# Projecting queries, keys and values in four groups, one per mLSTM head, with sample rows per head

## The chip, the cores and the metric

The kernel runs as one program on one core of one Trainium2 chip. The metric is the device time of one execution in microseconds (us). Work is shared between TensorE (PE in the profile; PEld is its weight load), VectorE (DVE), ScalarE (ACT), GpSimd (POOL, here mostly a second issuer of transfers) and SyncE (SP, which issues the weight loads).

## The reference

One layer of a hybrid decoder, for 256 prompt tokens and 8 sample tokens of one step each. One combined projection feeds two groups, an RG-LRU recurrence and an mLSTM with four heads; their outputs go through `w_out`. Then come a cross attention over 256 memory tokens and a gated feed-forward part.

```
xn = rmsnorm(x, g_mix)
z = xn @ w_in                      # rgx | rgg | q | k | v | o | i | f
xr, conv_new = causal_conv(z[..., OFF_RGX:OFF_RGG], ...)
h_rg, h_last = rglru(xr, r, i, lam, h0)          # a scan over time
y_rg = rmsnorm(h_rg * gelu(z[..., OFF_RGG:OFF_Q]), g_rg_out)
h_ml, C_new, n_new, m_new = mlstm(q, k * DK**-0.5, v, logi, logf, C0, n0, m0)
y_ml = rmsnorm(h_ml, g_ml_out) * sigmoid(z[..., OFF_O:OFF_I])
x = x + concat([y_rg, y_ml]) @ w_out
x = x + CrossAttn(rmsnorm(x, g_xa), mem k/v)
x = x + SwiGLU(rmsnorm(x, g_ffn))
y = rmsnorm(x, g_final)
```

For a prompt, a head of the mLSTM computes the products of its queries and keys (128 wide), weights them by gates, and multiplies with its values (256 wide). For a sample token it updates a 128 x 256 state C = dec C + k v, a normaliser n = dec n + k, and reads both with q. All states are outputs too.

## The kernel before

**Tiles.** The model dimension lies on the partitions, the 264 token columns (256 prompt, 8 sample) on the free axis. A weight block is 16 tiles of 128 x 128. Precision comes from splitting: ACT copies half a block (8 tiles) to fp32r (the high part, written `w<-raw` by ACT), DVE subtracts it from the raw data (the low part, `w<-raw,w` by DVE), and each tile is then used in three matmuls of 264 columns: high x high, high x low, low x high. So a block is a *step* of 48 matmuls in two *halves* of 24, and each half needs one pass of ACT and one of DVE. There are four buffers for split halves, so a split can begin when PE has left the half four before.

**Steps.** A list `steps` holds the blocks in the order in which PE takes them; the main loop near the end of the kernel runs over it. Steps 0 to 3 are the first four rgx blocks at once (a quarter of the depth each), 4 to 7 the other rgx blocks, 8 the gates (half as long), 9 to 16 the four q blocks and then the four k blocks, 17 to 24 the eight v blocks, 25 to 32 rgg, 33 to 40 o, 41 to 56 `w_out`. Then come `w_q`, the memory's keys and values, `w_o` and the feed-forward blocks. A block of `w_out` takes its first eight tiles from the recurrence (`yrg`), the last eight from the mLSTM (`yml`); the products with `yml` of its first blocks are asked for after the mLSTM's norm, so PE can take `yrg` halves of several blocks first.

**Accumulators.** A step ends with an evacuation (`evac_...`) of a PSUM bank that DVE or ACT reads. Of the eight banks `bank` gives four to `mm`, the steps, and four to `ax`, everything else; the first four rgx blocks use three `ax` and one `mm`.

**Side work.** All that is not a step is a generator, registered by `side(generator, prio)` and advanced by `pump` after each step. A `yield STEP` ends a generator's turn until the next step, `yield` with a number only offers a stop. `pump` goes through them by priority number and stops one that used DVE or ACT once that engine's planned clock is at the clock of PE plus a slack. `finish` runs them without such a limit. The planner then lays the recorded instructions out on each engine by a model of their times; each engine executes its own list in order. The side generators here:

- `rg_gen` (prio 0, from step 7): convolution, gates, exponentials and scans of the recurrence; a rgg step needs it to be done.
- `ml_gates` (0): gate values of the mLSTM, from step 8.
- `ml_prompt` (2), `ml_values` (2), `ml_heads` (2): transposed keys and the weighted q x k product of a head (`Pm`, with keys scaled in `kw`), transposed values, and the product of `Pm` and the values.
- `ml_sample` (3): the sample states. It writes k and q rows of the sample tokens to a scratch buffer `scr` in memory and reads them back broadcast over the partitions (`B<-scr`, with `c0T` for the old state). ACT forms products of k and v (`dw`), DVE the new state (`B<-B,bcs,dw`) and its dot products with q (`ds<-B,B`).
- `ml_norm` (6, from step 24): waits for heads and samples, sums over partitions by a matmul with ones (`ax<-ssum,ones`), finds the scale, scales `hT` (`B<-B,B` TENSOR_SCALAR), transposes it and forms `yml`.
- `mem_gen` (7, from step 40): the norm of the memory tokens, with an inverse root over a 128 x 256 tile in `rstd_wide`.

`evac_qk(7)`, the last k, starts `ml_sample`, `ml_prompt`, `ml_values` and `ml_heads`. `ml_prompt` transposes the keys of all heads into two banks and copies them to SBUF before the first head.

Of the kernel before, what the change touches and what calls it, by code (L numbers as in the profile page):

```python
# [17 lines left out]
P = 128  # L18
# [77 lines left out]
def layer_kernel(ctx: ExitStack, tc, xT, memT, vec, wrg, w_in, w_out, w_q, w_k, w_v, w_o,  # L96
# [236 lines left out]
    def bank(tag="mm"):  # L333
        return psm.tile([P, 512], F32, tag=tag, bufs=4, name=nm(tag))
# [390 lines left out]
    def evac_qk(j):  # L725
        def f(ps):
            if j == 0:
                ml["qk"] = Arr(8)
            if j < 4:
                dve.tensor_mul(halves(ml["qk"](j)), unturn(ps[:, :N]), halves(rstd))  # L730
            else:
                dve.scalar_tensor_tensor(halves(ml["qk"](j)), unturn(ps[:, :N]), KSCALE, halves(rstd),
                                         op0=OP.mult, op1=OP.mult)
# [40 lines left out]
    def ml_prompt():  # L774
        qk = ml["qk"]
        yield STEP
# [7 lines left out]
        while "gates" not in ml or not ml["gates"].done:  # L784
            yield STEP
        R = ml["R"]
        M = R(6)[:, :T]
        for h in range(H):
            sel = ident[:, h: h + 1].to_broadcast([P, P])
            bc = bank("ax")  # L790
            pe.matmul(bc[:, :T], sel, M, start=True, stop=True)
            sps = bank("ax")
# [4 lines left out]
            E, Pm, kw = w[:, 0:384], w[:, 384:768], ml["kb"][:, h].rearrange("p t d -> p (t d)")  # L797
# [12 lines left out]
            yield 1.0  # L810
            ml["pn"] = h + 1
# [44 lines left out]
    def ml_sample():  # L856
# [3 lines left out]
        ks, qs = qk.tile(1)[:, :, T:N], qk.tile(0)[:, :, T:N]  # L860
        sc, Dg = bcs[:, :, 0:8], bcs[:, :, 8:16]
        x = ltmp(64)
        kd, qc = (x[:, o: o + 32].rearrange("p (h b) -> p h b", b=NS) for o in (0, 32))
        dve.tensor_mul(kd, ks, Dg)
        dve.tensor_copy(qc, qs)
        n0 = V("n0", 0, 32).rearrange("p (h b) -> p h b", b=NS)
        dve.tensor_mul(snew, n0, sc)
        dve.tensor_add(snew, snew, kd)
        pool_e.dma_start(o_sn, snew)

        dve.tensor_mul(ssum[:, 1], snew, qc)
        yield 0.6
        yield STEP
        ps = bank("ax")
        pe.transpose(ps[0:64, 128:256], x, ident)
        yield STEP
        rows = ltmp(128)
        act.activation(rows[0:64, :], ps[0:64, 128:256], AF.Copy)
        scr = drm.tile([64, P], F32, name="scr")
        pool_e.dma_start(scr, rows[0:64, :])  # L880
        yield 0.5
        def fetch(h, b4):
            C, kq = B([P, 4, 2, P]), B([P, 2, 4, P])
            pool_e.dma_start(C, c0T[h, :, b4 * 4: b4 * 4 + 4])
            for j in range(2):
                r0 = j * 32 + h * 8 + b4 * 4
                src = scr[r0: r0 + 4, :].rearrange("b d -> (b d)")
                pool_e.dma_start(kq[:, j].rearrange("p b d -> p (b d)"), src.partition_broadcast(P))
            return C, kq

        ahead = fetch(0, 0)
        yield STEP
        for h in range(H):
            while ml.get("vn", 0) < 2 * h + 2 or "last" not in ml:
                yield STEP
            for b4 in range(2):
                C, kq = ahead
                n = 2 * h + b4 + 1
                if n < 2 * H:
                    ahead = fetch(n // 2, n % 2)  # L900
# [94 lines left out]
    first = [bank("ax"), bank("ax"), bank("ax"), bank()]  # L995
# [9 lines left out]
    def evac_first(_):  # L1005
        for n in (3, 0, 1, 2):
# [450 lines left out]
    for i, (src, cols, pef, evf, need) in enumerate(steps):  # L1457
# [174 lines left out]
```

## Time and profile before

| what | value |
|---|---|
| median of 3 runs | 1449.08 us (1449.05 to 1451.44) |
| the profiled execution | 1449.35 us |
| its span | 1447.4 us |
| mean granted TensorE clock | 0.999 |
| ACT busy | 793.9 us, 55% of the span |
| all DMA | 329.17 MB, 227 GB/s |

The execution's time is 1.95 us longer than its span, which begins and ends with its first and last instruction. "Busy" counts the instructions of an engine; where PE is busy in nearly the whole span, what matters is whether its matmuls follow each other at the pace of its long undisturbed stretches. In a timeline a row is a start, a length, engine, line, operation, operands, a count, and in brackets the idle time before it with what ended it. Names are those of the program's buffers: `w` a split half, `raw` its data, `mm` and `ax` accumulators, `B` and `t` working tiles. L61 is a line of a helper through which nearly all instructions are recorded, so groups are told apart by their names. A length in a timeline includes some overlap with the next instruction; differences of starts give the pace.

### The profile page before, as it was taken

Reading aid. Unit: us, or ns where it says so; the run is one execution under the profiler, and the core shown is the slowest. Engines: PE = TensorE matmul, PEld = TensorE weight load, DVE = VectorE, ACT = ScalarE, POOL = GpSimd, SP = SyncE. Lnnn points to the kernel's source line nnn. Section 1 sums busy time; section 2 is a strip of 40 time slices with the busy share of each in tenths; the row PEclk is TensorE's granted clock in tenths of the full one; section 3 lists DMA queues with packets and bytes.
Section 4 is the critical chain, followed back from the end, with each engine's and each line's share of the span. In section 5 each row is a group of like instructions: output and inputs, shape, how many; then the busy total and the mean of one; then the engine's idle time right before and its main releaser. Section 6 shows DMA issues by size and latency. Waiting matters only on the chain.

```text
span 1447.4 us, 29983 instructions
## 1 busy us (share of the span) xinstructions
PE 1432.6 (99%) x11987; PEld 1407.3 (97%) x11987; DVE 1046.6 (72%) x2007; ACT 793.9 (55%) x1286; POOL 127.8 (9%) x203
## 2 busy tenths in 40 slices
PE   9999999999999999999999999999999999999997
PEld 9999999999999999899999999999999999999997
DVE  7966798998899999977676665555656655556564
ACT  7678785765556666655544444434444443444463
POOL 0001220000225433300000000000000000000000
PEclk9999999999999999999999999999999999999999
DMA  9645897548799887856555555555555555555573
GB/s 288 235 174 184 295 372 272 179 173 276 277 336 376 322 306 258 340 172 216 193 196 196 192 201 192 197 196 192 200 192 195 199 192 198 193 193 200 164 240 126
DMA packets 100764, 329.17 MB, mean 227 GB/s; under 512 B 11056, under 2 KB 19936, under 8 KB 100624
## 3 DMA queue, kind: packets, MB, share of 16 engines
q1 hardware_dynamic: 84336, 271.95, 54.1%
q0 software_dynamic: 15424, 54.22, 10.1%
q8 instruction: 93, 1.52, 0.4%
q10 hardware_dynamic: 864, 1.09, 0.2%
q14 instruction: 47, 0.39, 0.1%
HBM read 314.36 MB, written 12.86 MB: 226 GB/s over the span
## 4 chain that ended last, share of the span: by engine, by line
PE 56%; DVE 1%; issue 1%; DMA 0%; POOL 0%; ACT 0%; DVEq 0%; POOLq 0%; ACTq 0%
PE mm L61 56%; PE ax L61 1%; DVE B L61 1%; DVE dw L61 0%; DMA o_v<-B 0%; POOL ds L1182 0%; DVE w L61 0%; ACT B L61 0%; DVE c L61 0%; ACT dw L61 0%; DVE t L61 0%; ACT ds L61 0%; DVEq L1609 0%; ACT c L61 0%; DVEq L61 0%
## 5 line engine op out<-in xcount | busy, mean ns | idle before, releaser
L61 PE MATMUL mm<-B,w 128*128 128x264 f32 (+1 forms) x10960 | 1282.2, 279 | 1.8 <-DVE w L61 1.7
L61 PEld LDWEIGHTS mm<-B,w 128*128 128x128 f32 x10960 | 1261.5, 189 | 9.9 <-DVE w L61 2.3
L61 DVE TENSOR_TENSOR w<-raw,w 128x1024 fp32r<-128x1024 f32 (+1 forms) x522 | 624.4, 1198 | 303.5 <-ACT w L61 302.7
L61 ACT ACTIVATE w<-raw 128x1024 fp32r<-128x1024 f32 (+1 forms) x522 | 534.9, 1028 | 512.2 <-PE mm L61 347.8
L61 PE MATMUL mm<-w,B 128*128 128x512 f32 x384 | 86.9, 380 | 0.1
L61 PEld LDWEIGHTS mm<-w,B 128*128 128x128 f32 x384 | 70.6, 189 | 9.8 <-DVE w L61 0.5
L1521 POOL TENSOR_TENSOR B<-B,rstd 128x264 f32<-128x264 f32 x4 | 2.8, 738 | 802.9 <-ACT rstd L61 802.9
L61 DVE TENSOR_TENSOR t<-mm,rstd 128x264 f32<-128x264 f32 x96 | 41.4, 432 | 28.4 <-PE mm L61 28.3
L61 DVE SCALAR_TENSOR_TENSOR B<-B,dw 128x256 f32<-128x256 f32 x128 | 55.0, 483 | 3.2 <-ACT dw L61 3.0
L61 DVE TENSOR_TENSOR xres<-xres,mm 128x264 f32<-128x264 f32 (+1 forms) x81 | 34.3, 425 | 27.0 <-PE mm L61 27.0
L61 DVE SCALAR_TENSOR_TENSOR dw<-B,qsm,dw 128x256 f32<-128x256 f32 x96 | 48.6, 511 | 2.6 <-ACT dw L61 1.8
L61 PE MATMUL ax<-B,B 128*128 128x256 f32 (+3 forms) x272 | 44.9, 305 | 1.1 <-DVE B L61 1.0
L1182 POOL TENSOR_TENSOR ds<-dw,ds 128x256 fp32r<-128x256 f32 x32 | 35.4, 1106 | 106.8 <-ACT ds L61 106.7
L61 PEld LDWEIGHTS ax<-B,B 128*128 128x128 f32 x272 | 37.9, 191 | 3.8 <-DVE B L61 1.6
L61 ACT ACTIVATE B<-xres,vecs 128x264 fp32r<-128x264 f32 (+1 forms) x64 | 32.2, 503 | 4.2 <-DVE xres L61 2.7
L61 ACT ACTIVATE dw<-B,qsm 128x256 f32<-128x256 f32 x32 | 16.2, 508 | 27.0 <-issue 13.9
L1171 POOL DMA_DIRECT2D B<-kcT x32 | 17.3, 541 | 139.6 <-DVE B L61 126.5
L61 ACT ACTIVATE t<-xres 128x264 f32<-128x264 f32 (+1 forms) x53 | 21.1, 409 | 15.3 <-DVE xres L61 15.2
L61 ACT ACTIVATE dw<-B,B 128x128 f32<-128x128 f32 x64 | 21.2, 393 | 11.2 <-DMA B<-scr 7.9
L61 DVE SCALAR_TENSOR_TENSOR B<-xres,vecs,B 128x264 fp32r<-128x264 f32 x48 | 23.4, 490 | 4.1 <-ACT B L61 4.1
L61 ACT ACTIVATE dw<-ax,dw 128x256 f32<-128x256 f32 x32 | 15.1, 471 | 19.3 <-DVE dw L61 18.3
L61 ACT ACTIVATE B<-t 128x264 fp32r<-128x264 f32 (+1 forms) x60 | 24.1, 409 | 2.1 <-DVE t L61 2.1
(176 smaller groups left out, 679.0 us busy)
## 6 DMA issues: line engine op xcount, KB each, us to landing
raw<-w_gu SPq DMA_DIRECT2D x176, 512.0 KB, 3.6
raw<-w_d SPq DMA_DIRECT2D x80, 512.0 KB, 3.6
raw<-w_in SPq DMA_DIRECT2D x74, 512.0 KB, 5.2
raw<-w_out SPq DMA_DIRECT2D x32, 512.0 KB, 3.7
raw<-w_q SPq DMA_DIRECT2D x32, 512.0 KB, 6.2
B<-kcT POOLq DMA_DIRECT2D x32, 512.0 KB, 8.8
B<-vcT POOLq DMA_DIRECT2D x32, 512.0 KB, 9.9
raw<-w_k SPq DMA_DIRECT2D x32, 512.0 KB, 5.0
```

The lines of the kernel that those rows point to most:

```text
L61: return f(*a, **k)
L1171: pool_e.dma_start(kc, kcT[h, b])
L1182: pool_e.tensor_sub(ws[:, 1], acc, ws[:, 0].bitcast(F32))
L1521: e.tensor_mul(st["y"](c), st["y"](c), r)
```

## The change

- The eight banks are divided into three `mm` and five `ax`; the first four rgx blocks are all in `ax`. At step 7 the evacuation of step 4, which is alone in `mm` by then, is put ahead of the three others that are waiting.
- Steps 9 to 24 are in the order q0 k0 v0 v1, q1 k1 v2 v3, q2 k2 v4 v5, q3 k3 v6 v7.
- The first k starts the side generators. The last k did so before.
- Sample rows are formed per head by a new generator, `ml_rows` (prio 2): five DVE operations on 8 columns, a transpose to 16 x 128, a copy by ACT and a transfer to the head's part of `scr`. Before, one such chain worked on 32 columns and 64 rows. `ml_sample` waits for a head's rows (`rn`) before it fetches them.
- `ml_prompt` waits for each head's key, transposes it into the second half of the bank that holds the head's gate row, and `kw` is scaled from there. The copies of all keys are gone.
- `ml_heads` has one more `yield STEP` between `Pm` and the product with the values.

The diff, in its core:

```
-        return psm.tile([P, 512], F32, tag=tag, bufs=4, name=nm(tag))
+        return psm.tile([P, 512], F32, tag=tag, bufs=3 if tag == "mm" else 5, name=nm(tag))
...
-            if j == 7:
+            ml["kn"] = j - 3
+            if j == 4:
+                side(ml_rows(), 2)
                 ml["sg"] = side(ml_sample(), 3)
                 side(ml_prompt(), 2)
                 side(ml_values(), 2)
...
-        kt, ml["kb"] = B([P, 2, H, P]), B([P, H, 2, P])
-        for tb in range(2):
-            ps = bank("ax")
-            for h in range(H):
-                pe.transpose(ps[:, h * P: h * P + P], qk(4 + h)[:, tb * P: tb * P + P], ident)
-            act.activation(kt[:, tb].rearrange("p h d -> p (h d)"), ps, AF.Copy)
...
+        for h in range(H):
+            while ml["kn"] <= h:
+                yield STEP
             yield STEP
...
+            bc, sps = bank("ax"), bank("ax")
+            kt = bc[:, T:].rearrange("p (t d) -> p t d", t=2)
+            pe.matmul(bc[:, :T], ident[:, h: h + 1].to_broadcast([P, P]), M, start=True, stop=True)
+            for tb in range(2):
+                pe.transpose(kt[:, tb], k[:, tb * P: tb * P + P], ident)
...
-            act.activation(kw[:, 0:P], kt[:, 0, h, :], AF.Copy, scale=E[:, 255:256])
-            act.activation(kw[:, P:T], kt[:, 1, h, :], AF.Copy, scale=E[:, 383:384])
+            for tb in range(2):
+                e = 255 + 128 * tb
+                act.activation(kw[:, tb], kt[:, tb], AF.Copy, scale=E[:, e: e + 1])
...
             while min(ml.get("pn", 0), ml.get("vtn", 0)) <= h:
                 yield STEP
             yield STEP
+            yield STEP
...
+    def ml_rows():
         while not ml["gates"].done:
             yield STEP
         qk = ml["qk"]
...
+        for h in range(H):
+            while ml["kn"] <= h:
+                yield STEP
+            x = ctile(2 * NS)
+            kd, qc = x[:, 0:NS], x[:, NS:]
+            dve.tensor_mul(kd, qk(4 + h)[:, T:N], bcs[:, h, NS:])
+            dve.tensor_copy(qc, qk(h)[:, T:N])
+            dve.tensor_mul(snew[:, h], V("n0", NS * h, NS), bcs[:, h, 0:NS])
+            dve.tensor_add(snew[:, h], snew[:, h], kd)
+            dve.tensor_mul(ssum[:, 1, h], snew[:, h], qc)
+            yield 0.3
+            yield STEP
+            ps = bank("ax")
+            pe.transpose(ps[0: 2 * NS, 0:P], x, ident)
+            yield STEP
+            rows = ltmp(P)[0: 2 * NS]
+            act.activation(rows, ps[0: 2 * NS, 0:P], AF.Copy)
+            pool_e.dma_start(scr[h], rows)
+            ml["rn"] = h + 1
+            yield 0.2
         pool_e.dma_start(o_sn, snew)
...
+                    while ml["rn"] <= n // 2:
+                        yield STEP
                     ahead = fetch(n // 2, n % 2)
...
-    first = [bank("ax"), bank("ax"), bank("ax"), bank()]
+    first = [bank("ax") for _ in range(4)]
...
-    for j in range(8):
-        proj(w_in[9 + j], rx, evac_qk(j))
-    for j in range(8):
-        proj(w_in[17 + j], rx, evac_v(j))
+    for h in range(H):
+        for j in (h, 4 + h):
+            proj(w_in[9 + j], rx, evac_qk(j))
+        for j in (2 * h, 2 * h + 1):
+            proj(w_in[17 + j], rx, evac_v(j))
...
+        if i == 7:
+            pend.insert(0, pend.pop(1))
```

What this moves is not written in the diff but comes out of the planner. Three places of the instruction lists show it, each before and after.

The first is PE at the turn into `w_out`. Before, `mm_3693` is block 1 and `mm_3843` block 2; `w_3629` is block 1's first half and `w_3632` its second, `B_3671` the high part of the first `yml` tile, and `ax` the transposes of the heads.

```order
L61 MATMUL mm_3693<-B_3321,w_3629 128x264
L61 MATMUL mm_3693<-B_3320,w_3629 128x264
L61 MATMUL ax_3718<-ident,B_2063 128x128 x4
L61 MATMUL ax_3731<-ident,B_2257 128x128 x4
L61 MATMUL ax_3746<-ident,B_2257 128x128 x4
L61 MATMUL mm_3635<-B_3671,w_3569 128x264
L61 MATMUL mm_3693<-B_3671,w_3632 128x264
L61 MATMUL mm_3843<-B_3245,w_3687 128x264
```

In the changed kernel `mm_3661`, `mm_3704` and `mm_3916` are blocks 0, 1 and 2, `w_3698` is the first half of block 2, and `B_3738` and `B_3739` are the high and low part of the first `yml` tile; `ax_3887` is the sum of the memory's norm.

```order
L61 MATMUL mm_3916<-B_3334,w_3698 128x264
L61 MATMUL mm_3916<-B_3333,w_3698 128x264
L61 MATMUL ax_3731<-ident,B_2212 128x128 x4
L61 MATMUL ax_3746<-ident,B_2212 128x128 x4
L61 MATMUL ax_3759<-ident,B_2628 128x128 x4
L61 MATMUL ax_3774<-ident,B_2628 128x128
L61 MATMUL ax_3887<-lt_3787,ones 128x256
L61 MATMUL ax_3774<-ident,B_2628 128x128 x3
L61 MATMUL mm_3661<-B_3738,w_3570 128x264
L61 MATMUL mm_3704<-B_3738,w_3658 128x264
L61 MATMUL mm_3916<-B_3738,w_3701 128x264
L61 MATMUL mm_3661<-B_3739,w_3570 128x264
```

The first products with `yml` stood after the first half of block 1 and were followed by the first half of block 2. They now stand after the first half of block 2, behind all transposes and the memory's sum.

The second place is DVE at the same turn. Before, `B_2063` and `B_2257` are the heads' `hT`, `B_3409` the scale, `B_3080` and `B_3412` the o gates, and `B_3672` the low part of the first `yml` tiles.

```order
L61 TENSOR_TENSOR nums<-nums,B_3409 128x4x8 x2
L61 TENSOR_SCALAR B_2063<-B_2063,B_3409 128x256 x4
L61 TENSOR_SCALAR B_2257<-B_2257,B_3409 128x256 x4
L61 TENSOR_TENSOR B_3080<-B_3080,nums 128x8 x3
L61 TENSOR_TENSOR B_3412<-mm_3572,rstd 128x264
L61 TENSOR_TENSOR B_3080<-B_3080,nums 128x8
L61 TENSOR_TENSOR B_3412<-B_3412,nums 128x8 x3
L61 TENSOR_TENSOR w_3632<-raw_3535,w_3632 128x8x128
L61 TENSOR_TENSOR B_3412<-B_3412,nums 128x8
L61 TENSOR_TENSOR B_3080<-B_3080,ax_3664 128x256 x2
L61 TENSOR_TENSOR w_3687<-raw_3621,w_3687 128x8x128
L61 SCALAR_TENSOR_TENSOR B_3672<-B_3080,vecs,B_3671 128x264 x2
```

After, from the same scaling on, `hT` is `B_2212` and `B_2628`, and the gates are `B_3094` and `B_3429`; `w_3910` is the first half of block 3.

```order
L61 TENSOR_SCALAR B_2212<-B_2212,B_3499 128x256 x4
L61 TENSOR_SCALAR B_2628<-B_2628,B_3499 128x256 x4
L61 TENSOR_TENSOR B_3094<-B_3094,nums 128x8 x4
L61 TENSOR_TENSOR B_3429<-B_3429,nums 128x8 x4
L61 TENSOR_TENSOR B_3094<-B_3094,ax_3731 128x256
L61 TENSOR_TENSOR w_3910<-raw_3686,w_3910 128x8x128
L61 TENSOR_TENSOR B_3094<-B_3094,ax_3731 128x256
L61 TENSOR_TENSOR B_3094<-B_3094,ax_3746 128x256 x2
L61 TENSOR_TENSOR B_3429<-B_3429,ax_3759 128x256 x2
L61 TENSOR_SCALAR t_3889<-ax_3887 128x256
L61 TENSOR_TENSOR B_3429<-B_3429,ax_3774 128x256 x2
L61 SCALAR_TENSOR_TENSOR B_3739<-B_3094,vecs,B_3738 128x264 x4
```

Some rows on, `lt_3834` is the memory's inverse root, `B_3690` to `B_3696` the memory tokens, and `w_3913` the second half of block 3.

```order
L61 TENSOR_TENSOR t_3890<-lt_3834 128x256
L61 SCALAR_TENSOR_TENSOR t_3890<-t_3890,t_3889 128x256
L61 SCALAR_TENSOR_TENSOR lt_3834<-t_3890,lt_3834 128x256
L61 TENSOR_TENSOR B_3690<-B_3690,lt_3834 128x256 x4
L61 TENSOR_TENSOR B_3692<-B_3692,lt_3834 128x256 x4
L61 TENSOR_TENSOR B_3694<-B_3694,lt_3834 128x256 x4
L61 TENSOR_TENSOR xres<-xres,mm_3661 128x264
L61 TENSOR_TENSOR B_3696<-B_3696,lt_3834 128x256 x3
L61 TENSOR_TENSOR xres<-xres,mm_3704 128x264
L61 TENSOR_TENSOR B_3696<-B_3696,lt_3834 128x256
L61 TENSOR_TENSOR w_3913<-raw_3688,w_3913 128x8x128
```

Additions of all gates with their transposes, then the memory's root and its sixteen products, now stand between the splits of block 3's halves; before, the memory's sums began behind the rows shown, and its products came later still.

The third place is ACT while the recurrence runs. Before, `lt_1801` is the row copy of all heads, `B_1539` and `B_1616` are tiles of the recurrence, `B_1707` the copied keys and `dw` the sample products.

```order
L61 ACTIVATE B_1539<-B_1539 128x264 x3
L61 ACTIVATE B_1616<-B_1616 128x264 x3
L61 ACTIVATE B_1707<-ax_1709 128x512
L61 ACTIVATE lt_1801<-ax_1715 64x128
L61 ACTIVATE w_1806<-raw_1693 128x8x128
L61 ACTIVATE w_1809<-raw_1695 128x8x128
L61 ACTIVATE B_1616<-B_1616 128x264
L61 ACTIVATE hlast<-B_1867 128x36
L61 ACTIVATE B_1707<-ax_1789 128x512
L61 ACTIVATE B_1625<-ax_1795 128x2x256
L61 ACTIVATE dw_1982<-B_1882,B_1636 128x128 x2
L61 ACTIVATE dw_2077<-B_1882,B_1636 128x128 x2
```

After, `lt_1581` is the row copy of the first head, `B_1568`, `B_966` and `B_1661` are tiles of the recurrence, `B_1507` is the first head's prompt weight, and `B_1192` its scaled keys.

```order
L61 ACTIVATE lt_1581<-ax_1498 16x128
L61 ACTIVATE B_966<-B_966,rgc 128x264
L61 ACTIVATE B_1568<-B_1568,ones 128x264
L61 ACTIVATE B_966<-B_966,rgc 128x264
L61 ACTIVATE B_1568<-B_1568,ones 128x264
L61 ACTIVATE B_966<-B_966,rgc 128x264
L61 ACTIVATE B_1568<-B_1568,ones 128x264
L61 ACTIVATE B_1507<-B_1507 128x384
L61 ACTIVATE w_1598<-raw_1482 128x8x128
L61 ACTIVATE B_1192<-ax_1500,B_1507 128x128 x2
L61 ACTIVATE w_1601<-raw_1484 128x8x128
```

A few functions of the recurrence later (`B_1661` and `B_1320` are its tiles too) the first sample products `dw` follow.

```order
L61 ACTIVATE B_966<-B_966,rgc 128x264
L61 ACTIVATE B_1568<-B_1568,ones 128x264
L61 ACTIVATE B_1320<-B_1320,rgc 128x264
L61 ACTIVATE B_1661<-B_1661,ones 128x264
L61 ACTIVATE dw_1677<-B_1593,B_1197 128x128 x2
```

The first head's rows, prompt weights and sample products have moved ahead of, and in between, functions of the recurrence that stood before them.

More of the change, by code (lines that the diff above doesn't have):

```diff
@@ L730, in f @@
                 dve.tensor_mul(halves(ml["qk"](j)), unturn(ps[:, :N]), halves(rstd))
-            else:
-                dve.scalar_tensor_tensor(halves(ml["qk"](j)), unturn(ps[:, :N]), KSCALE, halves(rstd),
-                                         op0=OP.mult, op1=OP.mult)
-            if j == 7:
+                return
+            dve.scalar_tensor_tensor(halves(ml["qk"](j)), unturn(ps[:, :N]), KSCALE, halves(rstd),
+                                     op0=OP.mult, op1=OP.mult)
+            ml["kn"] = j - 3
+            if j == 4:
+                side(ml_rows(), 2)
                 ml["sg"] = side(ml_sample(), 3)
@@ L775, in ml_prompt @@
         qk = ml["qk"]
-        yield STEP
-        kt, ml["kb"] = B([P, 2, H, P]), B([P, H, 2, P])
-        for tb in range(2):
-            ps = bank("ax")
-            for h in range(H):
-                pe.transpose(ps[:, h * P: h * P + P], qk(4 + h)[:, tb * P: tb * P + P], ident)
-            act.activation(kt[:, tb].rearrange("p h d -> p (h d)"), ps, AF.Copy)
+        ml["kb"] = B([P, H, 2, P])
+        while not ml["gates"].done:
             yield STEP
-        while "gates" not in ml or not ml["gates"].done:
+        M = ml["R"](6)[:, :T]
+        for h in range(H):
+            while ml["kn"] <= h:
+                yield STEP
             yield STEP
[L786 to L792, printed above, removed]
-            q, k = qk(h), qk(4 + h)
+            q, k = qk(h), qk(4 + h)
+            bc, sps = bank("ax"), bank("ax")
[3 more added lines that the diff above has]
+                pe.transpose(kt[:, tb], k[:, tb * P: tb * P + P], ident)
             pe.matmul(sps[:, 0:256], k[:, 0:P], q[:, 0:T], start=True, stop=True)
@@ L854, in layer_kernel @@
     nums = const.tile([P, 8, NS], F32, name="nums")
-    def ml_sample():
+    scr = drm.tile([H, 2 * NS, P], F32, name="scr")
+    def ml_rows():
         while not ml["gates"].done:
@@ L859, in ml_sample @@
         qk = ml["qk"]
[L860 to L868, printed above, removed]
-        pool_e.dma_start(o_sn, snew)
[L871 to L881, printed above, removed]
+        for h in range(H):
[18 more added lines that the diff above has]
+            yield 0.2
+        pool_e.dma_start(o_sn, snew)
+    def ml_sample():
+        sc = bcs[:, :, 0:NS]
         def fetch(h, b4):
@@ L885, in fetch @@
             for j in range(2):
[L886 to L887 removed]
+                r0 = j * NS + b4 * 4
+                src = scr[h, r0: r0 + 4, :].rearrange("b d -> (b d)")
                 pool_e.dma_start(kq[:, j].rearrange("p b d -> p (b d)"), src.partition_broadcast(P))
             return C, kq
+        while ml.get("rn", 0) < 1:
+            yield STEP
         ahead = fetch(0, 0)
@@ L1005, in evac_first @@
     def evac_first(_):
-        for n in (3, 0, 1, 2):
+        for n in range(4):
             evac_rgx(n)(first[n])
```

3 lines of the change are left out of this document (2 added, 1 removed).

## The prediction

> **What bounds the kernel now.** First the page's engine shares, then the windows, to see whether "PE busy" means PE at its pace.
>
> ```profile
> PE 1432.6 (99%) x11987; PEld 1407.3 (97%) x11987; DVE 1046.6 (72%) x2007; ACT 793.9 (55%) x1286; POOL 127.8 (9%) x203
> ```
>
> ```profile
> 1000.00:1400.00 400.00, 400.00 (x3558) 400.00 (x3557) 236.00 (x288) 179.94 (x221) 0.00 (x0) 1.00 0.57 196
> 190.00:200.00 10.00, 9.78 (x83) 9.34 (x82) 10.00 (x32) 8.67 (x22) 1.62 (x3) 1.00 1.02 381
> 200.00:210.00 10.00, 8.46 (x73) 8.14 (x72) 10.00 (x38) 8.43 (x19) 0.53 (x1) 1.00 0.96 380
> ```
>
> The columns after the length are PE, PEld, DVE, ACT and POOL, then the clock. In the long window PE does 3558 matmuls in 400 us: 0.1124 us each, so 48 of them (one step) take 5.40. Nothing in the change touches that stretch, so all of the answer lies where PE leaves this pace. The last two windows are such a place: DVE is full and PE is not.
>
> ```profile
> PE ax L61 <- DVE B L61: 2.0, 3, 1.0
> PE mm L61 <- DVE w L61: 1.7, 2, 1.5
> ```
>
> ```profile
> DVE t L61 <- PE mm L61: 28.3, 84, 0.4
> ```
>
> ```profile
> 96.18 5.65 PE L61 MATMUL mm<-B,w 128*128 128x264 f32 x48
> 101.66 1.94 PE L61 MATMUL ax<-B,B 128*128 128x264 f32 x8
> 103.25 16.56 PE L61 MATMUL mm<-B,w 128*128 128x264 f32 x144
> ...
> 140.77 0.66 PE L61 MATMUL ax<-ident,B 128*128 128x128 f32 x4 [1.00 <-DVE B L61]
> ...
> 208.61 16.24 PE L61 MATMUL mm<-B,w 128*128 128x264 f32 x142 [1.54 <-DVE w L61]
> ```
>
> In the lists of waits (total, times, longest) PE has three gaps where a side product of the mLSTM is asked of it before DVE has its operand, 2.0 us, and two where a weight split comes late, 1.7; PE's timeline puts the longest of each at 140.77 and 208.61. They show 3.7 us. The whole is larger. From 96.18, the start of step 15, to 208.61, the third matmul of step 32, lie 17 steps, 91.75 us at the pace, plus 0.22. Of side work the forms have 83 matmuls there, which I cost by differences of starts (eight of 264 columns 103.25 − 101.66 = 1.6, and so on): 12.8. That makes 200.95, so **7.7 us** of PE time is lost there. The 4.0 beyond the five gaps is the tail of the modelled ends (about 0.25 at each gap) and gaps the rows hide. That is all that can be won.
>
> **The change, part by part.** Grouping turns the order q q q q k k k k v... into q k v v four times. A first head has q, k and both values after step 12, where before its k came at 13 and its values at 18.
>
> *The three product waits go (part of the 7.7).* The extra step ahead of the product moves each one step, 5.4 us, later. The longest such wait showed 1.00, so Pm is ready. I count them as gone.
>
> *The two late splits (also in the 7.7) go, and what is late next.* They come from sample state work on DVE beside the splits, at 190 to 210. That work is not removed. By the order the second to fourth heads' rows still wait for the end of step 23, since the recurrence has precedence, and the state work ends half a step later than before.
>
> ```profile
> 183.07 1.22 DVE L61 TENSOR_TENSOR w<-raw,w 128x1024 fp32r<-128x1024 f32 x1
> 184.21 0.28 DVE L61 SCALAR_TENSOR_TENSOR ds<-B,B 128x128 f32<-128x128 f32 x1
> 184.42 0.08 DVE L61 DVE_READ_ACCUMULATOR ds<-B,B 128x1 f32 x1
> 184.42 0.43 DVE L61 TENSOR_TENSOR t<-mm,rstd 128x264 f32<-128x264 f32 x1
> 184.77 0.87 DVE L61 SCALAR_TENSOR_TENSOR B<-B,bcs,dw 128x256 f32<-128x256 f32 x2
> 185.56 0.28 DVE L61 SCALAR_TENSOR_TENSOR ds<-B,B 128x128 f32<-128x128 f32 x1
> ```
>
> ```profile
> L61 ACT ACT_TABLE_LOAD x16 | 20.5, 1283 | 2.0 <-PEq L1604 1.7
> ```
>
> Differences of starts give 1.14 for a split, 0.21 for a dot product of the state, 0.35 for an evacuation, 0.40 for a state update. Over the twelve splits of steps 28 to 33 the new order has 33 dot products, 19 updates, 16 operations of gate blocks and 1.6 us of the last head's prompt: 13.7 + 6.9 + 7.6 + 5.6 + 1.6 = 35.4, where the old one has 36 and 20 and no prompt work, 34.9. PE needs 36.0 there (twelve halves of 2.70 and 3.6 of side products). But ACT gets four more table loads in this part (20 for 16), 5.1 us, since the heads' exponentials now fall between gelus; I let half of it reach DVE, 38. DVE's lead over PE, about 6 us at the start by my count, shrinks to about 0.5 by the state work's end. The stall lies between 0 (the lead holds) and the 1.69 of before (nothing gained); I take **0.5**, near the lead's end.
>
> *A new stall in steps 19 to 22.* The first head's rows, prompt and two sample states are now pulled into the recurrence's stretch, where ACT has no room.
>
> ```profile
> 103.35:129.10 25.75, 25.75 (x231) 25.72 (x230) 13.65 (x28) 25.68 (x49) 1.67 (x3) 1.00 0.43 147
> ```
>
> ```profile
> 107.14 1.73 ACT L61 ACTIVATE B<-B,rgc 128x264 f32<-128x264 f32 x4
> 108.78 0.50 ACT L61 ACTIVATE B<-B,ones 128x264 f32<-128x264 f32 x1
> ...
> 126.68 0.25 ACT L61 ACTIVATE lt<-ax 64x128 f32<-64x128 f32 x1
> ...
> 136.24 1.28 ACT L61 ACTIVATE dw<-B,B 128x128 f32<-128x128 f32 x4 [4.11 <-DMA B<-scr]
> ```
>
> ```profile
> 126.90 2.15 DVE L61 TENSOR_TENSOR B<-B,B 128x264 f32<-128x264 f32 x6
> 128.96 1.85 DVE L61 TENSOR_TENSOR_SCAN B<-B,B 128x256 f32<-128x256 f32 x3
> ```
>
> ACT is busy 25.68 of 25.75 us before the change already. In the new order the row copy, one exponential, two scaled copies and twelve dw products stand in this stretch, ahead of the splits. From 103.35 to the split of step 21's second half I count 28.3 us of ACT: 24 recurrence functions 9.7 (0.41 each, 107.14 to 108.78), 8 splits 7.6 (0.95 each when back to back), 3 table loads 3.84, the 12 dw 3.6, and 3.6 of small ones. The dw products need rows that go to memory and back: 136.24 − 126.93 = 9.3 us from row copy to dw in this trace. With the row copy near 108.9 they arrive at 118.2, which costs ACT some 1.5 us of wait with splits behind it in the queue. Split 51 is then out of DVE at 134.75 and the next, behind seven products and five scans (5.6 us with the small ones, from the last two rows), at 141.5. PE wants the splits at 127.25 (gets 127.9: 0.65 lost) and, so delayed, at 139.1 (2.4 lost). **3.0**, between 1 and 5: less if the rows return early, more if the queue does not clear.
>
> *The turn into w_out.* Before, the mLSTM norm ends just in time and 262 matmuls run through.
>
> ```profile
> 247.65 0.33 PE L61 MATMUL ax<-ssum,ones 128*128 128x64 f32 x2
> ...
> 265.75 29.72 PE L61 MATMUL mm<-B,w 128*128 128x264 f32 x262
> ```
>
> ```profile
> 250.14 0.19 DVE L61 TENSOR_TENSOR B<-hden,hem 128x40 f32<-128x40 f32 x1
> ...
> 258.67 2.19 DVE L61 TENSOR_SCALAR B<-B,B 128x256 f32<-128x256 f32 x8
> ...
> 264.65 0.90 DVE L61 SCALAR_TENSOR_TENSOR B<-B,vecs,B 128x264 fp32r<-128x264 f32 x2
> ```
>
> The norm's sum over partitions runs on PE at 247.65, 11.0 us ahead of w_out's first block; from it to the first finished y tile lie 264.65 − 247.65 = 17.0 us. The new order puts that sum one step later, 5.4 ahead, and moves the memory norm's sums in between. So PE has taken the first (rg) halves of blocks 0, 1 and 2 and all 16 transposes with nothing left to fill, and waits for y. Call the start of block 0 zero. Splits come one a half, 2.7 apart, as PE frees their buffers, so DVE ends the split of block 2's second half at 7.7. Two products of nums and eight scalings (0.27 each) take it to 10.1 (258.67 shows them back to back), eight small products 0.8, a split 1.14, eight additions 2.8 and one more scaling 0.27 to 15.15, the first STT to 15.55. PE follows 0.2 later, as at 265.75 behind 264.65 + 0.90. Its own work, three halves of 2.70, 16 transposes and two sums, ends at 10.95: **4.8** lost. It then has 69 matmuls (7.75) and one half, to 26.2. Meanwhile DVE does the other seven STT and one scaling (3.1), the nine operations of the memory norm's inverse root (3.4, by 0.27 a scaling and 0.40 an STT) and its 16 products with two residual additions (6.2, by the 0.34 of the like ones at 126.90) before the next split: 29.4. That is **3.2** more. Together 8.0, between 5 and 10: 5 if the second wait is covered, 10 if the norm's small operations are spread by ACT's and PE's answers as before. The row of 262 shows 0 lost there now.
>
> *Smaller things.* Three more row transposes on PE: 0.3. Fifteen more small operations on DVE (0.2 each as at 250.14: 3.0, spread over steps 15 to 27, in whose first part DVE is busy 13.65 of 25.75 us) and three more row transfers issued by POOL on its own queue, which was busy 1.67 us in that window: 0, but each read of rows now queues behind them. The two bulk copies of keys on ACT go; that is inside the ACT count above. The bank move from mm to ax is 0: DVE stands waiting for PE 84 times in all (28.3 us, quoted), so an accumulator is emptied at once, and PE never waits for a bank in the list; if that cover went, PE would wait one evacuation, 0.35, a step.
>
> **Sum.** −7.7 + 3.0 + 0.5 + 8.0 + 0.3 = +4.1 us against the profiled execution's 1449.35 (span 1447.4 and 1.95 around it): 1453.45. The median of the three runs shown is 0.27 lower; I give **1453.2**.
>
> [...] The clock in every window quoted is 1.00, and the longest gap in them shows 1.54 us; no run here shows a longer one yet. [...]
>
> **The rivals.**
> - *R1, level.* The steps 19 to 22 stall vanishes (rows return before ACT asks), the turn stays. −7.7 + 0.5 + 8.0 + 0.3 = +1.1: **1450.2**. For it: the small early transfer meets a DMA share of only 0.43. Against: ACT is full there anyway.
> - *R2, faster.* DVE is ahead of its splits throughout: ACT's early queue clears in time, DVE's lead holds in steps 28 to 33, and the second wait at the turn is covered. It decides where DVE reaches that split 3.2 us earlier than counted. Then −7.7 + 0.3 + 4.8 = −2.6, and with DVE ahead by as much for the first wait too, 1.6 of it left, −5.8; between them **1445.0**. For it: the gaps to be won are measured, the new ones only counted from an order. Against: that order puts the 16 products ahead of the split.
> - *R3, slower still.* Row reads of heads 2 to 4 come late in steps 27 to 32, where the DMA share is 1.02 and a row fetch could take longer than the 9.3 above; ACT's queue has splits behind the dw products, so PE starves. It decides once a fetch is issued less than about 10 us ahead of its dw; one such wait as long as the 4.11 quoted adds it whole: **1457**.
> - *R4, the clock.* The 4.8 us gap at the turn is longer than any in the trace; if the granted clock falls behind it, PE's next half, 24 matmuls or 2.7 us at the pace, takes twice that: 1453.2 + 2.7, **1455.9**. For it: nothing in the trace excludes it. Against: gaps of up to 1.54 left the clock at 1.00. [...]
>
> **Chances.** Forecast 0.36 (its own range 1450.5 to 1455.5; 0.32 slower, 0.04 same), R1 0.24, R2 0.24, R3 0.09, R4 0.07. A measurement of this kernel tells 0.2%, 2.9 us, from no change. Faster 0.24, same 0.28, slower 0.48. The range 1445.5 to 1457.5 leaves half of R2's and some of R3's time outside.
>
> **What would show it.** In the new trace PE's three product waits should be gone; a wait of PE for w of 2 to 3 us between 127 and 142; one of 4 to 5 us just before the first product of w_out with yml, for B from DVE, and one of about 3 for a split some 10 us later. ACT's sample dw of the first head should wait for scr at about 117. I am wrong if PE runs through the turn (then faster), or if rows of the other heads are read late.

## The result and the profile after

The changed kernel takes 1470.17 us (median of 4 runs, 1469.38 to 1472.57) against 1449.53 us (4 runs): ratio 1.0142, with a 95% interval of 1.0130 to 1.0153. It is slower by 20.6 us where 4.1 us were forecast.

First the same lines of the page and of the list of waits, for the changed kernel.

```profile
PE 1441.0 (98%) x11990; PEld 1415.1 (96%) x11990; DVE 1049.9 (71%) x2022; ACT 799.2 (54%) x1291; POOL 127.4 (9%) x206
```

```profile
PE ax L61 <- ACT ds L61: 6.8, 3, 3.2
PE mm L61 <- DVE t L61: 3.2, 1, 3.2
PE mm L61 <- DVE B L61: 3.0, 1, 3.0
PE ax L61 <- DVE B L61: 2.9, 2, 2.7
```

The engines do nearly the work of before; the waits are other ones. The two longest groups did not exist before: PE waits for `ds`, which belongs to the sample tokens' attention over the memory, and for an evacuation `t`. Both lie far behind the code that the change reorders.

A way to see where the time goes is to compare the starts of one operation that both kernels do equally often: DVE's 522 weight splits, numbered from 0. The table gives the start in the timeline of before, and how much later (or earlier) the same split starts in others; the runs E1, E2, E11 and E13 are told below. A split's start also moves with DVE's own queue, so only differences that stay count.

| split | place | before | changed | E1 | E2 | E13 | E11 |
|---|---|---|---|---|---|---|---|
| 60 | v and rgg blocks | 165.3 | −5.4 | −2.9 | 0.0 | −0.1 | −4.8 |
| 92 | into `w_out` | 257.3 | +0.8 | +4.0 | +1.3 | +0.6 | −3.2 |
| 124 | end of `w_out` | 346.0 | +9.6 | +5.9 | +1.3 | +0.6 | −0.3 |
| 168 | second key block of the memory | 469.3 | +8.0 | +4.3 | +0.6 | +1.3 | −1.8 |
| 232 | `w_o` | 664.7 | +23.5 | +5.6 | +12.7 | +15.3 | −0.9 |

So the changed kernel is 5.4 us ahead at split 60, gives this back and 9 us more by the end of `w_out`, and loses another **15.5 us in the cross attention**, in which the diff changes nothing. Most of the lead at split 60 is not time won: from 96 us to that place PE's records have 36 matmuls of side work in the changed kernel and 69 before, so the others are still to come. The windows of the attention, before and then after:

```profile
465.00:690.00 225.00, 224.15 (x1488) 208.36 (x1487) 200.86 (x476) 140.05 (x271) 61.30 (x82) 1.00 0.74 272
```

```profile
465.00:690.00 225.00, 215.01 (x1326) 197.41 (x1325) 194.26 (x474) 134.88 (x262) 63.43 (x88) 0.98 0.73 267
```

PE's timeline of the changed kernel has, among others, these gaps (idle time before a row, and what ended it; one more, of 3.23 at 553.68, is shown further down):

```profile
140.93 0.90 PE L61 MATMUL ax<-ident,B 128*128 128x128 f32 x3 [2.70 <-DVE B L61]
...
215.61 8.14 PE L61 MATMUL mm<-B,w 128*128 128x264 f32 x70 [0.25 <-DVE w L61]
...
231.90 0.83 PE L61 MATMUL ax<-ident,c 128*128 128x128 f32 x6 [1.51 <-DVE c L61]
...
271.15 0.60 PE L61 MATMUL mm<-B,w 128*128 128x264 f32 x3 [0.60 <-ACT B L61]
274.79 10.98 PE L61 MATMUL mm<-B,w 128*128 128x264 f32 x69 [3.04 <-DVE B L61]
286.65 43.58 PE L61 MATMUL mm<-B,w 128*128 128x264 f32 x385 [0.87 <-DVE xres L61]
...
495.73 0.38 PE L61 MATMUL ax<-ds,onesr 128*128 128x256 f32 x1 [1.50 <-ACT ds L61]
504.95 0.38 PE L61 MATMUL ax<-ds,onesr 128*128 128x256 f32 x1 [2.08 <-ACT ds L61]
...
607.78 0.38 PE L61 MATMUL ax<-ds,onesr 128*128 128x256 f32 x1 [3.19 <-ACT ds L61]
```

And the windows behind three of its gaps:

```profile
141.00:144.00 3.00, 3.00 (x14) 3.00 (x15) 3.00 (x5) 1.66 (x3) 0.54 (x1) 0.50 0.63 202
274.80:279.80 5.00, 5.00 (x23) 5.00 (x24) 4.86 (x13) 0.20 (x1) 0.00 (x0) 0.50 0.00 1
506.00:509.00 3.00, 3.00 (x15) 2.72 (x14) 3.00 (x7) 1.05 (x3) 2.62 (x5) 0.53 1.00 333
```

PE is "busy" all of these windows, and does half the matmuls: the granted clock is 0.50. The clock record of this execution has five such stretches, 3.4, 6.8, 3.4, 3.4 and 3.4 us long, each beginning within 1.3 us of the end of one of the gaps. That is 20.5 us at half clock, or **10.2 us** lost beside the gaps themselves. This execution took 1472.57 us, the longest of the four, at a mean granted clock of 0.992; the others have 0.995 to 0.996, so by an estimate from these means they lost about half as much in this way.

### The profile page after: what moved, and what is told of

It reads as the page before. It is cut to its first block, busy times and chain, and to the rows that moved or that the text cites. A ratio compares the mean times of both kernels' runs of the same rounds, so it can differ in the third digit from the quotient of the medians.

```text
span 1470.9 us, 30043 instructions
## 1 busy us (share of the span) xinstructions
PE 1441.0 (98%) x11990; PEld 1415.1 (96%) x11990; DVE 1049.9 (71%) x2022; ACT 799.2 (54%) x1291; POOL 127.4 (9%) x206
## 4 chain that ended last, share of the span: by engine, by line
PE 58%; DVE 1%; issue 0%; ACT 0%; DVEq 0%
PE mm L61 57%; PE ax L61 1%; DVE B L61 0%; DVE dw L61 0%; ACT B L61 0%; DVE c L61 0%; DVE w L61 0%; DVEq L1621 0%; ACT ds L61 0%; ACT c L61 0%; DVEq L61 0%
## 5 line engine op out<-in xcount | busy, mean ns | idle before, releaser
L61 PE MATMUL mm<-B,w 128*128 128x264 f32 (+2 forms) x10912 | 1276.9, 280 | 8.0 <-DVE t L61 3.2
L61 DVE TENSOR_TENSOR xres<-xres,mm 128x264 f32<-128x264 f32 (+1 forms) x81 | 34.2, 424 | 28.3 <-PE mm L61 28.3
L61 DVE SCALAR_TENSOR_TENSOR B<-B,dw 128x256 f32<-128x256 f32 x128 | 51.5, 455 | 1.5 <-ACT dw L61 1.5
L61 PE MATMUL ax<-B,w 128*128 128x264 f32 x192 | 23.0, 280 | 2.2 <-ACT w L61 2.2
```

What stands on the lines that cost most here:

```text
L61: return f(*a, **k)
```

## The experiments

Medians are set against runs of the kernel before on the same chip, between 1449.85 and 1450.55.

**E1, the banks back at four and four.** This is the changed kernel with:

```
-        return psm.tile(..., bufs=3 if tag == "mm" else 5, ...)
+        return psm.tile(..., bufs=4, ...)
-    first = [bank("ax") for _ in range(4)]
+    first = [bank("ax"), bank("ax"), bank("ax"), bank()]
-        if i == 7:
-            pend.insert(0, pend.pop(1))
```

> The changed kernel with the banks back at four mm and four ax (first accumulators and the evacuation of step 4 as before); all the rest of the change stays. Theory A, three mm banks are too few: in the cross attention the value blocks hold two banks for four steps, and at the turn into w_out no fourth block can fill the wait. Then the 14 to 15 us that the changed kernel loses between splits 168 and 232 vanish, and most of the 9 to 10 us lost near split 96: 1446 to 1450 us. Theory B, the loss at the turn comes from the later mLSTM norm and the memory sums beside it, and the attention loss from work that was displaced by the new order: 1465 to 1471. If only the attention loss belongs to the banks: about 1456.

Measured 1453.50, ratio 1.0024 (1.0014 to 1.0033). The attention costs what it cost before (split 168 to 232: +4.3 to +5.6). At the turn PE has a fourth block to work on, and of the 3.04 a 0.90 is left, after 22 to 24 matmuls of that block:

```profile
142.22 0.90 PE L61 MATMUL ax<-ident,B 128*128 128x128 f32 x3 [4.01 <-DVE B L61]
...
274.39 3.22 PE L61 MATMUL mm<-B,w 128*128 128x264 f32 x24 [0.90 <-ACT B L61]
```

So the banks are 17 of the 20.6 us. It fell short of the 1446 to 1450 of theory A because the first gap is still there, and larger: 4.01, and from 142.0 to 148.5 the granted clock is 0.53. The three transposes and 96 matmuls behind the gap take 14.07 us by their starts, where in E3, told below, the same take 11.19 behind a gap of 2.71. So this gap costs about 6.9 us in this execution, where in the changed kernel 2.70 and 3.4 us at half clock cost 4.4. Why it grew with four banks is not shown.

**E2, only the banks, on the kernel before.** The same lines the other way round.

> The kernel before with only the bank part of the change: three mm, five ax, the first four accumulators in ax, step 4 evacuated first. Theory A: the attention loss appears, about 14 us, and little at the turn, since there the y tiles are ready early: 1462 to 1466 us. Theory B: 1449 to 1451.

Measured 1463.51, ratio 1.0095 (1.0078 to 1.0112), with the changed kernel's waits in the attention:

```profile
PE ax L61 <- ACT ds L61: 6.3, 3, 2.7
PE mm L61 <- DVE t L61: 3.2, 1, 3.2
```

Three banks for the steps bring the attention's loss by themselves (12.1 us from split 168 to 232), and nothing at the turn (no change from split 92 to 124), where the y tiles come early in the old order. One other wait is new, 2.61 at 178.29, and the six products behind it take 2.39 us, where six like them at 162.97 take 1.12; at split 92 only 1.3 us of all this are left.

**E3, one accumulator of each memory value block in ax**, in the changed kernel.

```
-                kv["vps"] = [bank(), bank()]
+                kv["vps"] = [bank(), bank("ax")]
```

> The changed kernel (three mm, five ax) with one of the two accumulators of a memory value block taken from ax. Theory A in the narrow form, that a value block holds two of three mm banks: the loss in the attention goes, the one at the turn stays: 1454 to 1458 us. If it is not the value blocks but some other shortage or the displaced order: 1468 to 1472.

Measured 1476.11, ratio 1.0174 (1.0158 to 1.0189). Neither expectation held: the attention became worse, and PE's wait for `ds` rose to 15.4 us in five places, the longest 5.8. Why is not shown; the accumulator now sits in the group that the decode products (`ax<-ds,onesr`) take their banks from. So the run neither confirms the narrow form nor rules out a shortage.

**E8 and E12, releasing the value accumulators early**, both on E2. E8 lets ACT copy each accumulator once and makes the split from the copy; E12 also takes the tiles for it two steps earlier.

```
-                act.activation(halves(vh), ps, AF.Copy)
-                dve.tensor_sub(halves(vv[1][:, tb, :]), ps, halves(vh.bitcast(F32)))
-                act.activation(halves(vf[:, tb, :]), ps, AF.Copy)
+                act.activation(halves(vf[:, tb, :]), ps, AF.Copy)
+                act.activation(vh, vf[:, tb, :], AF.Copy)
+                dve.tensor_sub(vv[1][:, tb, :], vf[:, tb, :], vh.bitcast(F32))
```

> The kernel before with three mm and five ax, and a memory value block's accumulators read once by ACT and released, the split being made from that copy. Theory A, the loss in the attention comes from value blocks that hold two of three banks until ACT, DVE and ACT have read each: released by the first read, the 11 to 13 us of loss shrink to under half, 1450 to 1456. Theory C, it is the number of banks as such, whenever they are released, or the order laid out around it: 1461 to 1466.

> The kernel before with three mm and five ax, the early release of the value accumulators, and the tiles that they are copied to taken two steps earlier, so that the copy does not wait for a working tile. Theory A, value accumulators held too long: 1451 to 1457. Theory C, the number of banks or the order laid out around it: 1461 to 1466.

Measured 1464.22 and 1464.77 (ratios 1.0093 and 1.0094). By the numbers this is theory C, but neither did what it was for. ACT's first read of the second value block comes 12.8 us after the end of its last matmul in both, against 9.9 in E2, since the copy stands behind other work; both banks are free only 13.9 us after that end, against 15.8. They leave open whether a truly early release would help.

**E13, one bank for the keys with four and four.** The kernel before, in which a value block takes a third bank and gives it back after its accumulators have been read.

```
+                kv["third"] = bank()
+                pe.matmul(kv["third"][:, 0:P], ident, ident, start=True, stop=True)
...
+                if tb == 1:
+                    act.activation(tmp(T)[:, 0:8], kv["third"][:, P:P + 8], AF.Copy, scale=vf[:, 1, 0:1])
```

> The kernel before with its four and four banks; a memory value block takes a third bank and holds it until its accumulators have been read (two extra matmuls of 128 columns and one small copy a block, under 1 us in all). So the key blocks have one bank while a value block waits to be read, as with three mm banks, and everything else keeps four. Theory A, one bank for the keys is the loss in the attention: 1460 to 1466, with waits of PE for a key evacuation and for rows of the decode products, as in the runs with three banks. Theory C, the loss needs the five ax banks or three banks elsewhere: 1450 to 1453.

Measured 1464.48, ratio 1.0102 (1.0085 to 1.0118); 13.9 us are lost from split 168 to 232. Of PE's waits there the longest is 4.53; three more show 1.20 to 1.81, and none is for a key evacuation by DVE:

```profile
493.03 0.58 PE L61 MATMUL ax<-ds,onesr 128*128 128x256 f32 x1 [4.53 <-ACT ds L61]
...
496.64 3.64 PE L61 MATMUL mm<-B,w 128*128 128x512 f32 x15 [0.26 <-ACT B L61]
```

The loss needs neither five ax banks nor three elsewhere. A single bank left to the key blocks brings it back, as theory A said, though with other waits.

**E4, the memory norm four steps later**, with four and four banks (`if i == 44` for 40).

> The changed kernel with four and four banks, and the memory norm started after step 44 instead of 40, so that its sums and products leave the turn into w_out. Theory A: a fourth block fills PE's wait there already, so the time is that of the run with four and four banks alone, within 1.5 us. Theory B: the memory's work on DVE at the turn is the loss, so this one is 5 to 9 us faster than that run.

Measured 1453.20, ratio 1.0017 (1.0007 to 1.0026), against E1's 1453.50, as theory A said: the memory's work at the turn is not what costs there once a fourth block can fill. With three banks this was not tried.

**E5 and E6, the first gap**, with four and four banks. E5 puts a `yield STEP` ahead of the value transposes in `ml_values`; E6 also takes the change's step in front of the product away.

> The changed kernel with four and four banks, and one more step ahead of the transposes of a head's values. Theory A: what the grouped order still loses with four and four banks is one wait of 4.0 us of PE for values that DVE evacuates behind the recurrence's scans, with 6.8 us at half clock behind it (3.4 us more). Asked for a step later, the values are ready: 1445 to 1448 us. Theory B, DVE and ACT are simply too full in steps 19 to 22 and another wait (a split) takes its place: 1452 to 1455.

> As the run before it, and without the step in front of the product. Theory A: the step's worth is the waits for Pm, 2 to 3 us with their tails, against a norm that ends one step earlier at the turn, where the run with four and four banks loses 2.5 us: within 2 us of the run before it, faster if the waits for Pm do not come back. Theory B, the step is what hides the products: 3 us or more slower than the run before it.

Measured 1452.72 (ratio 1.0020, 1.0010 to 1.0029) and 1451.38 (1.0007, 0.9998 to 1.0017). The wait for values goes, and a split is late in its place. In E5 (E6 has the same 2.57 at 141.93):

```profile
141.96 7.11 PE L61 MATMUL mm<-B,w 128*128 128x264 f32 x46 [2.57 <-DVE w L61]
```

For E5 that is theory B: another wait takes the place of the first, as if DVE were too full there. E6 lies 1.3 us below E5, within the 2 us of its theory A, and has no wait for `Pm`, so the step in front of the product is not what hides the products in the grouped order.

**E7, the first head's rows held until the recurrence is done** (E1 with a wait for `rg` in `ml_rows`).

> The changed kernel with four and four banks, and the first head's rows (and with them the sample states) held until the recurrence is done. Theory A (the late values): DVE has fewer small operations there, but the transposes are still asked for as early; the 4.0 us wait shrinks at most by the sample's work, 1450 to 1454. Theory B (the sample work pulled into the recurrence is the cause, as predicted): the early wait goes and the time is 1445 to 1449, unless the sample's end delays the turn.

Measured 1463.23, ratio 1.0094. The early wait fell to 0.54, and the turn paid: 2.69, 2.32 and 1.72 of PE for late splits and y tiles between 265 and 299, and the matmuls there are slow: 22 from 267.22 and 22 from 273.82 take 0.19 us each, and 96 from 283.28 take 13.1 us, against 10.8 at the pace of 0.1124. That fits states which, begun one row round trip later, end too late; the end itself was not traced to these waits.

**E11 and E14, the states held, not their rows.** E11 is E6 with

```
         ahead = fetch(0, 0)
         yield STEP
+        while not st["rg"].done:
+            yield STEP
```

> The grouped order with four and four banks, the step ahead of the value transposes, none in front of the product, and the sample states (not their rows) held until the recurrence is done, so that DVE has no sample work in the recurrence's stretch. Theory A, the sample work pulled in there makes the split late (2.6 us and 1.7 of half clock in the run with the same steps): 1446 to 1449, if the states still end before the turn. Theory B, they end later and the turn pays, as with rows held back: 1453 to 1464.

> As the run with four and four banks and the sample states held until the recurrence is done, but with the change's step in front of the product. Theory A, the step only moves the norm 5.4 us towards the turn, where that run waits 1.7 us already: 1 to 3 us slower, 1449 to 1451. Theory B, the step hides late products: the same or faster, 1446 to 1448.

E11 measured **1447.90**, ratio 0.9981 (0.9972 to 0.9990): the one version that beats both kernels, by 2.7 us. Its longest gap shows 1.15 and the mean granted clock of its profile is 0.999, as before:

```profile
PE mm L61 <- DVE w L61: 2.5, 4, 1.1
PE mm L61 <- ACT w L61: 1.1, 1, 1.1
```

E14, the same with the step in front of the product, measured 1449.26, ratio 0.9997 (0.9988 to 1.0006): in the range of theory A, though the two intervals overlap, and no gain of that step can be seen.

**E9 and E10, the step alone**, on the kernel before: in front of the product (E9), and ahead of the value transposes too (E10).

> The kernel before with one part of the change alone, the step in front of the product with the values. Theory A: the waits of PE for Pm (0.39 and 0.65 shown, about 1.5 with their tails) go, and the rest of the state work shifts with them: 1446 to 1449. Theory B, the product then asks for DVE's time later, where the sample states fill it, and the norm comes a step later at the turn: 1450 to 1455.

> As the run before it, and a step ahead of the value transposes. Theory A: the wait of 1.00 for values goes too, 1 to 1.3 us less than the run before it. Theory B: it comes back as a late split, so no difference.

Measured 1449.55 (0.9997, 0.9988 to 1.0006) and 1450.36 (1.0001, 0.9992 to 1.0009): no change, so theory B of E10, and for E9 neither theory. In E9 one product wait is 1.26, and four late splits appear at 185 to 217: one kind of wait went and another came.

## Why the prediction was wrong

**The step that failed is the banks.** It said that "the bank move from mm to ax is 0: DVE stands waiting for PE 84 times in all (28.3 us, quoted), so an accumulator is emptied at once, and PE never waits for a bank in the list". The row is true, and is about `t<-mm,rstd`, accumulators that DVE is waiting to read. It says nothing of those that nobody is waiting to read. A memory value block uses two accumulators over four steps. In the trace of before, PE and ACT around the second one:

```profile
523.46 4.27 PE L61 MATMUL mm<-w,B 128*128 128x512 f32 x19
```

```profile
542.05 1.08 ACT L61 ACTIVATE B<-mm 128x512 fp32r<-128x512 f32 x2
...
550.81 1.08 ACT L61 ACTIVATE B<-mm 128x512 f32<-128x512 f32 x2 [1.13 <-DVE dw L61]
```

The last product ends near 527.7, the first read comes at 542.1, the last ends at 551.9: both banks are held for **24 us** after the work. With four banks, two are left to the key blocks; with three, one. The changed kernel shows it at the same place:

```profile
549.31 1.15 PE L61 MATMUL mm<-B,w 128*128 128x512 f32 x6
553.68 6.05 PE L61 MATMUL mm<-B,w 128*128 128x512 f32 x25 [3.23 <-DVE t L61]
```

```profile
551.45 0.36 ACT L61 ACTIVATE t<-mm 128x256 f32<-128x256 f32 x1
...
553.30 1.08 ACT L61 ACTIVATE B<-mm 128x512 fp32r<-128x512 f32 x2 [0.57 <-DVE dw L61]
```

```profile
553.12 0.41 DVE L61 TENSOR_TENSOR t<-t,mm 128x256 f32<-128x256 f32 x1
```

PE goes on when the key block's own evacuation by DVE ends at 553.5, before the value accumulators have been read. The other waits, for `ds`, come with another order: the product that waits 3.19 at 607.78 stands 96 matmuls of the steps earlier than in E1 (by the counts of recorded matmuls, corrected by the 48 by which they differ ahead of the attention). The likely reading is that the planner lays PE's decode products ahead of a key block that has no bank, and on the chip their operands are late. In the changed kernel's trace the three waits for `ds` are 6.8 us, the wait for the evacuation 3.2, and the three half-clock stretches behind them 5.1: 15.1 of the 15.5. E1, E2 and E13 show the cause; how a single bank leads to each wait is in part argued. The prediction looked for a bank wait only in the trace of before, which has four, and only in the part that the diff names; its price for the case that the cover went, 0.35 a step, was too small for what came.

**The turn into `w_out`** was forecast to 0.3 us at its first wait: y due 15.75 us after the start of block 0, which by its rows began near 259.25, so at 275.0; PE went on at 274.79. The second wait, 3.2 for a split, did not show. In its place the half clock took its 69 matmuls from 7.75 to 10.98 us, and 0.87 went to a bank that waited for block 0's evacuation. Forecast 8.0, measured 8.8 from split 92 to 124: the first wait came as reasoned, but that the sum is near is luck, since a loss at half clock stands where a wait for a split was forecast. "Nothing left to fill" was right, and its cause was missed: E1 fills it with a fourth block, so this loss too is mostly the banks'.

**Steps 19 to 22** were forecast at 3.0 (1 to 5) with the stall at 139.1. The gap came at 138.2 to 140.9 and shows 2.70, with 1.7 of half clock behind it: the right place, and about 4.4. What PE waited for is a value's evacuation behind scans on DVE:

```profile
139.86 0.69 DVE L61 TENSOR_TENSOR_SCAN B<-B,B 128x256 f32<-128x256 f32 x1
140.46 0.41 DVE L61 TENSOR_TENSOR B<-mm,rstd 128x264 f32<-128x264 f32 x1
```

The step's rows were wrong, so the nearness of 2.70 to 3.0 is luck in part: the round trip took no longer than ACT needed (row copy 108.63, first dw 116.47, no wait), and the instruction that waited was a value transpose, not a split. With the states held back the longest wait there is 1.15 (E11) where it is 2.57 with the same steps (E6), so the states' early start is at fault.

**The waits to be won** (7.7) were won only in part. The product waits are gone; E6 and E11 have none either, without the step in front of the product, so that comes with the grouped order. But by the forecast's terms PE should reach `w_out` 3.9 us ahead (−7.7 + 3.0 + 0.5 + 0.3). The sum over partitions, which stands one step of 5.40 later, starts there:

```profile
253.71 0.33 PE L61 MATMUL ax<-ssum,ones 128*128 128x64 f32 x2
```

Before, it started at 247.65, so PE is 0.7 behind. Of these 4.6 us the first gap is 1.4 (4.4 for 3.0), a wait of 1.51 at 231.90 for the scale of the recurrence's norm, which no term had, is another part, and the rest, about 1.7 us, must be loss that was counted as winnable and stayed.

**Steps 25 to 34** were forecast at 0.5; a single 0.25 showed at 215.61.

**R4, the clock**, was one of five cases and given 0.07. It came beside the other losses, five times: 10.2 us. It was tied to the gap of 4.8 us at the turn, and gaps that show 2.08 to 3.23 us were enough. Its price, one half of a step at twice its time, was the author's assumption, which no run of before shows; in the changed kernel 23 matmuls fill the 5.00 us from 274.80 at a clock of 0.50, 0.217 each against 0.1124, and the half clock lasts 3.4 or 6.8 us at a time.

## What to carry to other kernels

Before a buffer count is lowered, list for every accumulator in the whole program how long it is held between its last matmul and its last read, not only in the part that is edited, and count the banks that this leaves free at the worst place. An absent wait in a trace proves only that the present count is enough. A wait of PE as long as the five here, 2.08 to 3.23 us, must be priced with the half-clock stretch that can follow it: in the changed kernel's trace five gaps of 14.2 us together were followed by 10.2 us lost at half clock.

## What the runs showed of the hardware

From 4.39 to 1440 us the clock record of the changed kernel's profile shows two values, 1.00 and 0.50. The half clock begins at 140.93, 274.05, 506.15, 553.94 and 608.55 and lasts 3.41 us, at 274.05 6.83. Between these stretches lie 129.71, 225.28, 44.37 and 51.20 us at full clock: 38, 66, 13 and 15 times the shortest stretch, 3.413 us, to within 0.03 us. In the 3.41 us ahead of the five falls PE is idle for 2.70, 2.82, 2.08, 3.15 and 2.64 us in all; behind the gaps that show 1.51 at 231.90 and 1.50 at 495.73 the clock stays at 1.00.

The length of a single gap does not decide whether the matmuls behind it are slow. Three pairs show nearly the same gap in two runs, with different times behind it, taken from the starts of PE's rows:

| behind the gap | longer | shorter |
|---|---|---|
| three transposes and 96 matmuls | changed kernel, gap 2.70: 12.83 us | E3, gap 2.71: 11.19 us |
| 14 side products and 44 matmuls of the attention | changed kernel, gap 2.08: 10.53 us | E2, gap 2.08: 8.87 us |
| the key matmuls up to the next decode product, 19 in E12 | E8, gap 3.31: 4.90 us | E12, gap 3.31: 3.24 us |

The differences are 1.64, 1.66 and 1.66 us. In the first two pairs the clock record of the changed kernel has 3.41 us at 0.50 there, which costs 1.7 by an estimate, half of that time. What sorts the cases was not shown; no run moved a gap on purpose.
